# Value products of a cached-attention side stream issued in pairs behind its score products, and empty steps added to an mLSTM side stream

## The chip, the cores and the metric

One core of one Trainium2 chip runs the whole program as one launch. The metric is the device time of that core in microseconds (us).

## The reference, cut to what matters

One decoder layer is applied to 2048 new prompt tokens and to 64 sampled tokens (8 sequences of 8). It projects the tokens once, runs two groups of heads, and then an output projection and an MLP with layer norms. All data are float32.

```python
# sampled tokens, forgetting attention over a paged cache of 8192 past tokens, 8 heads of 64
k_past = cache_k[l][page_table].reshape(DB, past, FOX_HEADS, FOX_HEAD_DIM)
v_past = cache_v[l][page_table].reshape(DB, past, FOX_HEADS, FOX_HEAD_DIM)
s_past = einsum('bqhd,bkhd->bhqk', q, k_past) * scale + Ln[..., :, None] + R[:, :, None, :]
s_new  = einsum('bqhd,bkhd->bhqk', q, k_new) * scale + Ln[..., :, None] - Ln[..., None, :]
p = softmax(concatenate([s_past, where(causal, s_new, -inf)], -1))
o = einsum('bhqk,bkhd->bqhd', p[..., :P], v_past) + einsum('bhqk,bkhd->bqhd', p[..., P:], v_new)
...
# mLSTM, 4 heads of 128, one chunk (the prompt is scanned in chunks, a sample is one chunk)
C_new = g_state * C + einsum('bhs,bshd,bshe->bhde', w_key, k, v)     # state
n_new = g_state * n + einsum('bhs,bshd->bhd', w_key, k)              # normaliser
...
x1 = layer_norm(DN_ALPHA * x + mix @ w_o)
y  = layer_norm(DN_ALPHA * x1 + square(relu(x1 @ w1)) @ w2)
```

## The kernel before

**Main work.** Four stages follow each other: A (input projections of four blocks of 512 prompt tokens; the sampled tokens ride with the first), B (forgetting attention of the prompt), O (output projection) and C (the MLP, again in four blocks). A float32 product of the main work is split into a high and a low part, so that it becomes three matrix products (`mm3`, L157 to L159) of 128 rows by 256 to 512 columns. These are most of TensorE's instructions, and are called big matmuls below.

**Two side streams run beside it.** They are Python generators. The main work calls `tick(us)` after each of its units; `tick` adds `us` to two accounts, and each time an account passes its pace, the generator of that account takes one step (up to its next `yield`).

- The *m stream* (`macc`, pace `PACE_M` = 2.3) holds a list: `gate_stream(bi)` (gate rows of block bi), `m_block(bi)` (the mLSTM chunks of block bi, four chunks of 128 tokens, seven or eight steps each) and, after block 0, `m_sample()` (the mLSTM of the sampled tokens). When block bi+1 reaches its convolutions, it steps the m stream until `m_block(bi)` is done (`while mst.get("open")` in `block_a`), and only then goes on.
- The *attention stream* (`sample_attention`, pace 5.6 in stage A and 5 in stages O and C, nearly none in B) does the sampled tokens' attention over the cache. It has 294 steps; 32 of them belong to one of the 8 samples.

**The attention stream's step n** (`step(n)`) holds, in this order: turning gathered keys on VectorE (`k_turn`, L1674); every fourth step the scores of four gathered key pieces (`qk_step`, L1697: 16 products in 128x32 tiles); once a sample the softmax (`softmax`, L1716 and the exponentials L1734); every second step one value product (`pv_step` of p, L1809: 8 products in 128x32 tiles, p = 0 to 127, 16 to a sample); the end of a sample (`pv_end`, L1824); the new tokens' part (`softmax_new`, L1746) and the sum (`softmax_sum`, L1754); transposes of the weights (`weights(b, u, hg)`, L1766, two calls for each fourth of a sample, copied by ScalarE and VectorE at L1768); and at its end the gathers for later steps (`v_gather`, L1785, and `k_gather`, L1668, indirect DMAs issued by GpSimd).

A value product needs its gathered values in SBUF. There are two places for them: place 0 (two `vt` buffers) always, place 1 only while the main work lends buffers (`vx["more"]`, from stage O on, given back at each block's end). `v_gather` runs when a place is free, on odd steps, or at once when no place is in use. Scores fall on steps n with n % 4 == 2, value products with even p on the same steps behind the scores, and those with odd p on n % 4 == 0.

**The order on each engine** is written when the program is built: the Tile framework takes the instructions with their order of issue as a priority and places each by its own estimate of when its operands are ready. Within an engine that order is fixed at run time. So a step given later in the program moves an instruction only if the framework's estimate did not already put it there.

Of the kernel before, what the change touches and what calls it, by code (L numbers as in the profile page):

```python
# [52 lines left out]
def body(ctx, tc, I, O, stages):  # L53
# [51 lines left out]
    vx = dict(more=None, live=[], next=0, of={})  # L105
# [255 lines left out]
    def gate_stream(bi):  # L361
# [43 lines left out]
        def rowset(cols, base, n_el, np_, sample):  # L405
            R = [pa.tile([8, 1024], F32, name="rows", tag="xn", bufs=2) for _ in range(2)]
            fr = R[1][:, 0:n_el]
            yield 1
            V.tensor_copy(fr, rows([c[0] for c in cols], 8, np_))
            if sample:  # L410
                V.tensor_tensor_scan(fr, rm8, fr, 0.0, op0=OP.mult, op1=OP.subtract)
            else:
                V.tensor_tensor_scan(fr, ones8.to_broadcast([8, 512]), fr, 0.0 if bi == 0 else Lend, op0=OP.mult, op1=OP.subtract)
                V.tensor_copy(Lend, fr[:, 511:512])
            SY.dma_start(dnl[:, base:base + n_el], fr)
            ir = R[0][0:4, 0:n_el]
            yield 1
            V.tensor_copy(ir, rows([c[1] for c in cols], 4, np_))
            lr = R[0][0:4, 512:512 + n_el]
            yield 1  # L420
            V.tensor_copy(lr, rows([c[2] for c in cols], 4, np_))
            mr = R[1][0:4, 0:n_el]
            br = R[1][0:4, 512:512 + n_el]
            if sample:
                V.tensor_tensor_scan(br, rm8[:4], lr, 0.0, op0=OP.mult, op1=OP.add)
                for b in range(8):
                    s = slice(b * 8, b * 8 + 8)
                    V.tensor_tensor_scan(mr[:, s], lr[:, s], ir[:, s], smT[:, b:b + 1], op0=OP.add, op1=OP.max)
                m0 = [smT[:, b:b + 1] for b in range(8)]
                cl = 8  # L430
                mo = O["m_sample"].rearrange("l b h -> h (l b)")
            else:
                for c in range(4):
                    s = slice(c * 128, c * 128 + 128)
                    V.tensor_tensor_scan(br[:, s], ones8[:4].to_broadcast([4, 128]), lr[:, s], 0.0, op0=OP.mult, op1=OP.add)
                V.tensor_tensor_scan(mr, lr, ir, 0.0 if bi == 0 else mend, op0=OP.add, op1=OP.max)
                cl = 128

            V.tensor_tensor(lr, mr, br, op=OP.subtract)
            V.tensor_tensor(ir, ir, br, op=OP.subtract)  # L440
            SY.dma_start(dM[:, base:base + n_el], lr)
            for c in range(n_el // cl):
                s = slice(c * cl, c * cl + cl)
                if sample:
                    m0 = smT[:, c:c + 1]
                elif c == 0:
                    m0 = None if bi == 0 else mend
                else:
                    m0 = mr[:, c * cl - 1:c * cl]
                if m0 is None:  # L450
                    V.tensor_scalar(br[:, s], lr[:, s], -1.0, None, op0=OP.mult)
                else:
                    V.tensor_scalar(br[:, s], lr[:, s], -1.0, m0, op0=OP.mult, op1=OP.add)
            SY.dma_start(dar[:, base:base + n_el], br)
            ge = pa.tile([4, 8], F32, name="ge", bufs=1)[:, :n_el // cl]
            V.tensor_copy(ge, br.rearrange("p (c t) -> p c t", t=cl)[:, :, cl - 1])
            if sample:
                SY.dma_start(dgs_s, ge)
                me = pa.tile([4, 8], F32, name="me", bufs=1)
                V.tensor_copy(me, mr.rearrange("p (c t) -> p c t", t=cl)[:, :, cl - 1])  # L460
                SY.dma_start(mo, me)
            else:
                SY.dma_start(dgs[:, bi * 4:bi * 4 + 4], ge)
                V.tensor_copy(mend, mr[:, 511:512])
                if bi == 3:
                    SY.dma_start(O["m_prompt"].rearrange("l b h -> h (l b)"), mend)
            if bi == 0 and not sample:
                yield 1

            for i, c in enumerate(cols):  # L470
                yield 1
                s = slice(i * np_, (i + 1) * np_)
                pg = ppm.tile([128, 8], F32, name="mg", tag="mm", bufs=2)[:np_]
                T.transpose(pg[:, 0:4], ir[:, s], ident[:4, :4])
                T.transpose(pg[:, 4:8], mr[:, s], ident[:4, :4])
                V.tensor_copy(c[3], pg)
# [3 lines left out]
        if pre:  # L480
            yield from rowset([(gnats[:, 0:8], gats[:, 8:12], gnats[:, 8:12], gms)], S, 64, 64, True)
# [342 lines left out]
    def m_sample():  # L824
# [67 lines left out]
        for h in range(4):  # L892
# [32 lines left out]
            for q in range(2):  # L925
                vx = pm.tile([64, 4, 128], F32, name="vx", tag="va", bufs=2)
                V.tensor_tensor(vx, va[:, h, None, 0:128].to_broadcast([64, 4, 128]),
                                bm[:, q * 4:q * 4 + 4, None].to_broadcast([64, 4, 128]), op=OP.mult)
                yield 1
                pc = ppm.tile([128, 4, 128], F32, name="mm", tag="mm", bufs=2)  # L930
                T.matmul(pc, kw[:, h], vx, start=True, stop=True)
                for b in range(4):
                    bb = q * 4 + b
                    V.scalar_tensor_tensor(C0[:, bb], C0[:, bb], gsb[:, h, bb:bb + 1], pc[:, b], op0=OP.mult, op1=OP.add)
# [3 lines left out]
            T.matmul(pn2, kw[:, h], bm, start=True, stop=True)  # L938
            V.tensor_tensor(n1[:, :, h], n0[:, :, h], gsb[:, h], op=OP.mult)
            V.tensor_tensor(n1[:, :, h], n1[:, :, h], pn2, op=OP.add)  # L940
        yield 1
        pe = ppm.tile([32, 128], F32, name="mm", tag="mm", bufs=2)
        T.transpose(pe, n1.rearrange("p b h -> p (b h)"), ident)
# [587 lines left out]
def sample_attention(tc, I, O, ps_, pps, cst, ident, sqk, dnl, dR, dmix, dqb, vx, kx, pe, ring_a):  # L1531
# [84 lines left out]
    for g in range(2):  # L1616
        p = pps.tile([32, 8, 64], F32, name="sT", tag="sX", bufs=1)
# [174 lines left out]
    def pv_step(b, kt, after):  # L1792


        z = state[b]
        if kt == 0:
            z["po"] = pps.tile([128, 256], F32, name="sO", bufs=1)
        po = z["po"]
        pg = kt % 4
        vts = vx["of"].pop(b * 16 + kt)  # L1800
        vx["live"].pop(0)
        for n, f in enumerate((1, 0)):
            with ExitStack() as es:
                if after is not None:
                    es.enter_context(tc.issue_after(after.ins))
                for g in range(2):
                    for hg in range(2):
                        r = (g * 2 + hg) * 32
                        after_ = T.matmul(po[r:r + 32], z["PT"][:, hg, 2 * f + g, pg].rearrange("p h q -> p (h q)"),  # L1809
                                          vts[f][:, g, hg * 256:(hg + 1) * 256], start=(kt == 0 and n == 0),  # L1810
                                          stop=(g == 1 and kt == 15 and n == 1), skip_group_check=True)
            after = after_
        if kt == 15:
            for hg in range(2):
                T.matmul(po[hg * 32:hg * 32 + 32], z["pn"][:, hg], z["vn"][:, hg * 256:(hg + 1) * 256],
                         start=False, stop=True, skip_group_check=True)
            z["os"] = ps_.tile([128, 256], F32, name="os", bufs=1)
            V.tensor_scalar(z["os"], po, z["rl"], None, op0=OP.mult)

    def pv_end(b):  # L1820
        z = state.pop(b)
# [11 lines left out]
    def at(n, first, of):  # L1833

        i, r = divmod(n - first, of)
        return i if r == 0 and i >= 0 else None
# [4 lines left out]
    def step(n):  # L1841
        after = None
# [11 lines left out]
        if g is not None and g < 64:  # L1854
            after = qk_step(g)
        b = at(n, 35, 32)
        if b is not None and b < 8:
            softmax(b)
        p = at(n, 38, 2)
        if p is not None and p < 128:  # L1860
            pv_step(p // 16, p % 16, after)
        b = at(n, 69, 32)
        if b is not None:
            pv_end(b)
        b = at(n, 37, 32)
        if b is not None and b < 8:
            softmax_new(b)
            v_new(b)
        b = at(n, 40, 32)
        if b is not None and b < 8:  # L1870
            softmax_sum(b)
        for hg in range(2):
            u = at(n, 36 + hg, 8)
            if u is not None and u < 32:
                weights(u // 4, u % 4, hg)
        b = at(n, 30, 32)
        if b is not None and b < 7:
            q_load(b + 1)
        b = at(n, 3, 32)
# [12 lines left out]
        if NA + 6 <= n < 256:  # L1892
            k_gather(n)

    for n in range(294):
        yield 1
        step(n)
        if n == NA + 2:

            yield 3  # L1900
            for i in range(6):
                k_gather(NA + i)
                if i < 5:
                    yield 1
# [23 lines left out]
```

## Time and profile before

| | |
|---|---|
| time, median of 3 runs | 3322.77 us (3321.24 to 3331.57) |
| the profiled execution's own time | 3348.73 us, of which its span is 3347.0 us |
| granted TensorE clock over the span | 0.989 |
| instructions in the span | 57284 |

A page of the profile gives each engine's busy time; a group of instructions (line of the kernel, engine, operation, output<-inputs) gives a count, the busy time, the mean of one, and the idle time of the engine just before the group with what ended it. PE is TensorE's matmul, PEld its weight load, DVE is VectorE, ACT ScalarE, POOL GpSimd. A float32 product in a 128x32 tile leaves two records, so the 8 products of a `pv_step` show as x16 and the 16 of a `qk_step` as x32. In a timeline, a row's first number is its start, and the step from one start to the next is what an instruction costs TensorE, because durations overlap.

### The profile page before, as it was taken

Reading aid. Unit: us, or ns where it says so; the run is one execution under the profiler, and the core shown is the slowest. Engines: PE = TensorE matmul, PEld = TensorE weight load, DVE = VectorE, ACT = ScalarE, POOL = GpSimd, SP = SyncE. Lnnn points to the kernel's source line nnn. Section 1 sums busy time; section 2 is a strip of 40 time slices with the busy share of each in tenths; the row PEclk is TensorE's granted clock in tenths of the full one; section 3 lists DMA queues with packets and bytes.
Section 4 is the critical chain, followed back from the end, with each engine's and each line's share of the span. In section 5 each row is a group of like instructions: output and inputs, shape, how many; then the busy total and the mean of one; then the engine's idle time right before and its main releaser. Section 6 shows DMA issues by size and latency. Waiting matters only on the chain. (4 is left out here: it accounts for less than half of the span.)

```text
span 3347.0 us, 57284 instructions
## 1 busy us (share of the span) xinstructions
PE 3224.8 (96%) x21420; PEld 2634.7 (79%) x21420; DVE 2130.2 (64%) x5161; ACT 1355.5 (40%) x2670; POOL 929.7 (28%) x1060
## 2 busy tenths in 40 slices
PE   9999999999999999999999999999999999999998
PEld 8998897787877777676777777777776777889997
DVE  6857567556478777656666667666676545755555
ACT  4443344334367777312332333232332333433332
POOL 0112122322344444465323324323243210100001
PEclk9999999999999999999999999999999999999999
DMA  5666765867642223787877768767668654542221
GB/s 174 167 190 190 220 205 189 288 215 226 220 122 84 77 82 114 246 274 242 296 241 250 247 232 298 253 224 270 211 238 304 198 172 142 160 138 79 89 85 66
DMA packets 427294, 646.22 MB, mean 193 GB/s; under 512 B 83149, under 2 KB 320017, under 8 KB 426121
## 3 DMA queue, kind: packets, MB, share of 16 engines
q1 hardware_dynamic: 350184, 363.09, 35.9%
q0 software_dynamic: 74304, 270.57, 22.0%
q10 hardware_dynamic: 2528, 8.91, 0.7%
q8 instruction: 169, 2.77, 0.3%
q14 instruction: 109, 0.89, 0.1%
HBM read 589.63 MB, written 52.83 MB: 192 GB/s over the span
## 5 line engine op out<-in xcount | busy, mean ns | idle before, releaser
L1489 DVE TENSOR_TENSOR y<-y,py 128x512 f32<-128x512 f32 x475 | 320.6, 682 | 313.5 <-PE py L159 276.9
L149 ACT ACTIVATE wh<-wr 128x1024 fp32r<-128x1024 f32 x268 | 279.4, 1056 | 523.7 <-PE py L159 207.1
L1668 POOL DMA_INDIRECT kT<-cache_k,idxK x256 | 269.1, 1051 | 725.5 <-PE sQ L1697 657.7
L159 PE MATMUL ph<-x1h,wl 128*128 128x512 f32 (+1 forms) x1280 | 452.6, 355 | 9.5 <-DVE wl L152 8.3
L157 PE MATMUL ph<-x1h,wh 128*128 128x512 f32 (+1 forms) x1280 | 454.7, 355 | 4.0 <-ACT wh L149 2.2
L158 PE MATMUL ph<-x1l,wh 128*128 128x512 f32 (+1 forms) x1280 | 454.5, 355 | 1.6 <-issue 1.6
L1674 DVE STREAM_TRANSPOSE kT<-kT 128x512 f32<-128x512 f32 x512 | 330.3, 685 | 182.2 <-DMA kT<-cache_k,idxK 171.6
L157 PE MATMUL py<-wh,h 128*128 128x512 f32 x1024 | 407.0, 400 | 4.4 <-DVE y L1487 2.3
L159 PE MATMUL py<-wh,h 128*128 128x512 f32 x1024 | 401.6, 393 | 1.0 <-issue 1.0
L158 PE MATMUL py<-wl,h 128*128 128x512 f32 x1024 | 401.5, 393 | 1.1 <-issue 1.0
L152 DVE TENSOR_TENSOR wl<-wr,wh 128x1024 fp32r<-128x1024 f32 x268 | 336.8, 1263 | 89.2 <-PE ph L159 35.2
L157 PE MATMUL pm<-whi,xhT 128*128 128x256 f32 (+2 forms) x1040 | 303.4, 292 | 3.2 <-issue 2.0
L158 PE MATMUL pm<-wlo,xhT 128*128 128x256 f32 (+2 forms) x1040 | 298.1, 287 | 0.0
L159 PE MATMUL pm<-whi,xlT 128*128 128x256 f32 (+2 forms) x1040 | 297.9, 286 | 0.0
L159 PEld LDWEIGHTS ph<-x1h,wl 128*128 128x128 f32 x1280 | 241.7, 189 | 45.6 <-DVE wl L152 10.5
L157 PEld LDWEIGHTS ph<-x1h,wh 128*128 128x128 f32 x1280 | 241.5, 189 | 42.0 <-issue 4.7
L158 PEld LDWEIGHTS ph<-x1l,wh 128*128 128x128 f32 x1280 | 241.8, 189 | 37.8 <-issue 6.4
L157 PEld LDWEIGHTS py<-wh,h 128*128 128x128 f32 x1024 | 192.5, 188 | 59.4 <-issue 11.9
L159 PEld LDWEIGHTS py<-wh,h 128*128 128x128 f32 x1024 | 192.5, 188 | 46.9 <-issue 5.8
L158 PEld LDWEIGHTS py<-wl,h 128*128 128x128 f32 x1024 | 192.7, 188 | 37.4 <-issue 2.3
L1785 POOL DMA_INDIRECT vt<-cache_v,idxV x158 | 161.5, 1022 | 201.0 <-PE sO L1809 140.2
L157 PEld LDWEIGHTS pm<-whi,xhT 128*128 128x128 f32 (+1 forms) x1040 | 199.1, 191 | 11.5 <-issue 8.8
(420 smaller groups left out, 6627.5 us busy)
## 6 DMA issues: line engine op xcount, KB each, us to landing
wr<-w SPq DMA_DIRECT2D x256, 512.0 KB
wra<-w_in SPq DMA_DIRECT2D x112, 512.0 KB
Rb<-dR SPq DMA_DIRECT2D x128, 128.0 KB
wr<-w_o SPq DMA_DIRECT2D x16, 512.0 KB
xr<-dmix SPq DMA_DIRECT2D x16, 512.0 KB
y<-x_prompt SPq DMA_DIRECT2D x16, 512.0 KB
dx<-y SPq DMA_DIRECT2D x16, 512.0 KB
xr<-dx SPq DMA_DIRECT2D x16, 512.0 KB
```

The source lines that it names most:

```text
L149: last["ACT"] = A.activation(dst, src, AF.Copy, scale=scale)
L152: r = (eng or V).tensor_tensor(dst, src, hi.bitcast(F32), op=OP.subtract)
L157: T.matmul(ps, wh, xh, start=first, stop=False)
L158: T.matmul(ps, wh, xl, start=False, stop=False)
L159: last["PE"] = T.matmul(ps, wl, xh, start=False, stop=stop)
L1489: V.tensor_tensor(y, y, ps, op=OP.add)
L1668: G.indirect_dma_start(out=piece(n), out_offset=None, in_=ck, in_offset=IO(ap=idxK[:, b, j // 2, j % 2:j % 2 + 1], axis=0))
L1674: V.transpose(x, x)
L1785: G.indirect_dma_start(out=vt.rearrange("p f c -> p (f c)"), out_offset=None, in_=cv, in_offset=IO(ap=idxV[:, b, (kt % 4) * 4 + kt // 4, f ...
```

## The change

Attention stream: a value product with even p is followed in the same step by the one with odd p, if its gather has been issued; `done` remembers how far the products have come, so that the odd one is not done again. Products whose partner has not been gathered are done alone as before. The new tokens' part moves from step 37 to 39 of a sample, the sum from 40 to 41, and both transposes of a sample's first fourth go to step 37 (they were at 36 and 37).

m stream: one more empty step in `gate_stream` of block 0, ahead of the transposes of its prompt rows; one ahead of each of the eight state products of `m_sample` (four heads, two halves); one ahead of its normaliser's transpose.

```diff
             if bi == 0 and not sample:
+                yield 1
                 yield 1
...
                 V.tensor_tensor(vx, va[:, h, None, 0:128].to_broadcast([64, 4, 128]),
                                 bm[:, q * 4:q * 4 + 4, None].to_broadcast([64, 4, 128]), op=OP.mult)
                 yield 1
+                yield 1
                 pc = ppm.tile([128, 4, 128], F32, name="mm", tag="mm", bufs=2)
                 T.matmul(pc, kw[:, h], vx, start=True, stop=True)
...
+        yield 1
         yield 1
         pe = ppm.tile([32, 128], F32, name="mm", tag="mm", bufs=2)
         T.transpose(pe, n1.rearrange("p b h -> p (b h)"), ident)
...
             V.tensor_scalar(z["os"], po, z["rl"], None, op0=OP.mult)
+        return after
...
         p = at(n, 38, 2)
-        if p is not None and p < 128:
-            pv_step(p // 16, p % 16, after)
+        if p is not None and p < 128 and p >= done[0]:
+            after = pv_step(p // 16, p % 16, after)
+            done[0] = p + 1
+            if p % 2 == 0 and p + 1 in vx["of"]:
+                pv_step(p // 16, p % 16 + 1, after)
+                done[0] = p + 2
...
-        b = at(n, 37, 32)
+        b = at(n, 39, 32)
         if b is not None and b < 8:
             softmax_new(b)
             v_new(b)
-        b = at(n, 40, 32)
+        b = at(n, 41, 32)
         if b is not None and b < 8:
             softmax_sum(b)
         for hg in range(2):
             u = at(n, 36 + hg, 8)
-            if u is not None and u < 32:
+            if u is not None and u < 32 and u % 4:
                 weights(u // 4, u % 4, hg)
+            u = at(n, 37, 32)
+            if u is not None and u < 8:
+                weights(u, 0, hg)
...
+    done = [0]
     for n in range(294):
         yield 1
         step(n)
```

## The prediction

> **What bounds the kernel.** I read the page first, for the engine that is full; then the groups of the lines that the change touches, by whole run and in stage A alone; then the timeline of TensorE around single bursts of the attention stream, since the page's averages can't price a change of order; and last the instruction order of both kernels as built, which tells what moves.
>
> ```profile
> span 3347.0 us, 57284 instructions
> ...
> PE 3224.8 (96%) x21420; PEld 2634.7 (79%) x21420; DVE 2130.2 (64%) x5161; ACT 1355.5 (40%) x2670; POOL 929.7 (28%) x1060
> ```
>
> TensorE is busy for 96% of the span and no other engine comes near. Every instruction keeps its work, so time can only come from two places: the idle 122 us (3347.0 less 3224.8), or the extra steps that TensorE spends where it goes over from one kind of product to another.
>
> The groups, each with its count, busy time, mean, and the idle time just before it with what ended it; the first row is of the stretch from 240 to 915 us alone, the others of the whole run:
>
> ```profile
> L1809 PE MATMUL sO<-vt,PTs 128*32 128x256 f32 x336 | 26.3, 424 | 15.8 <-DMA vt<-cache_v,idxV 15.8
> ...
> L1809 PE MATMUL sO<-xr,PTs 128*32 128x256 f32 x672 | 47.9, 382 | 0.6 <-DMA xr<-cache_v,idxV 0.6
> L1809 PE MATMUL sO<-vx,PTs 128*32 128x256 f32 x112 | 7.3, 380 | 0.0
> L1766 PE MATMUL sT<-ident,S 128*128 128x128 f32 x256 | 40.8, 280 | 7.4 <-ACT S L1734 4.1 <-ACT PTs L1768 2.9 <-DVE mxs L1704 0.3
> L931 PE MATMUL mm<-vx,kws 64*128 64x512 f32 x16 | 9.0, 641 | 2.2 <-DVE vx L927 1.7 <-ACT num L916 0.5
> L943 PE MATMUL mm<-ident,n 128*32 128x128 f32 x1 | 0.3, 284 | 1.8 <-DVE n L940 1.8
> L474 PE MATMUL mg<-ident,rows 4*128 4x4 f32 (+1 forms) x17 | 3.0, 209 | 2.4 <-DVE rows L440 2.4
> L802 PE MATMUL mn<-va,kw 128*128 128x129 f32 x128 | 19.5, 275 | 3.4 <-ACT hh L728 1.8 <-issue 1.6
> ```
>
> Sixteen records make one value product. In stage A 21 products (336 records) run with one place only, and there TensorE waits 15.8 us for their gathers, 0.75 us each. From the lent buffers (xr and vx) come 42 + 7 = 49 products with 0.6 us of waits: where two places exist, the values are there in time. The new order has 50 pairs, all in stages O and C, and leaves the 28 others alone; so the pairing does nothing for the 15.8 us.
>
> **Pairs.** What a product costs alone, between big matmuls:
>
> ```profile
> 2262.41 0.39 PE L159 MATMUL ph<-x1h,wl 128*128 128x512 f32 x1
> 2262.72 1.07 PE L1809 MATMUL sO<-xr,PTs 128*32 128x256 f32 x16
> 2263.72 0.50 PE L157 MATMUL py<-wh,h 128*128 128x512 f32 x1
> 2264.07 0.40 PE L158 MATMUL py<-wl,h 128*128 128x512 f32 x1
> 2264.31 0.40 PE L159 MATMUL py<-wh,h 128*128 128x512 f32 x1
> 2264.54 0.40 PE L157 MATMUL py<-wh,h 128*128 128x512 f32 x1
> 2264.77 0.40 PE L158 MATMUL py<-wl,h 128*128 128x512 f32 x1
> ```
>
> and what it costs as the second of a pair behind scores, which happens by chance already:
>
> ```profile
> 2432.90 1.93 PE L1697 MATMUL sQ<-kT,qb 128*32 128x256 f32 x32
> 2434.65 1.05 PE L1809 MATMUL sO<-vt,PTs 128*32 128x256 f32 x16
> 2435.51 1.05 PE L1809 MATMUL sO<-xr,PTs 128*32 128x256 f32 x16
> 2436.49 0.50 PE L159 MATMUL py<-wh,h 128*128 128x512 f32 x1
> ```
>
> Read the starts. The plain step of a big matmul is 0.23 (2264.54 to 2264.77). Going into the lone product takes 0.31, the product 1.00, the first big matmul behind it 0.35. From 2262.41 to 2264.77 it is 2.36 us; less five plain steps (1.15), 1.21 us. In the pair the product steps from 2434.65 to 2435.51, and the way out is as long as it is behind a lone one: 0.86 us. So a lone product that is moved behind another saves 0.35 us.
>
> How many move: in the old order 67 runs of value products start straight behind a big matmul, in the new one 35. That is 32 x 0.35 = 11.2 us. Against this, weight transposes that used to stand behind the odd product are now entered from a big matmul (20 stood behind a product, now 4):
>
> ```profile
> 2405.93 0.39 PE L158 MATMUL ph<-x1l,wh 128*128 128x512 f32 x1
> 2406.16 0.60 PE L1766 MATMUL sT<-ident,S 128*128 128x128 f32 x4
> 2406.52 0.48 PE L159 MATMUL ph<-x1h,wl 128*128 128x512 f32 x1
> 2406.83 0.40 PE L157 MATMUL py<-wh,h 128*128 128x512 f32 x1
> ...
> 2284.40 0.66 PE L1766 MATMUL sT<-ident,S 128*128 128x128 f32 x4
> 2284.81 0.47 PE L157 MATMUL ph<-x1h,wh 128*128 128x512 f32 x1
> 2285.12 0.39 PE L158 MATMUL ph<-x1l,wh 128*128 128x512 f32 x1
> ```
>
> Alone, the transposes take 0.36 and the big matmul behind them 0.31 instead of 0.23: 0.44. Behind a product they take 0.41, and the big matmul behind them 0.31 where it would be 0.35 behind the product: 0.37. So 16 x 0.07 = 1.1 us come back, and 10.1 remain. A second count gives the lower end: all interruptions of the big matmuls, whoever makes them, go from 544 to 521, and 23 x 0.35 = 8.1. I take 9, with 8.1 and 10.1 as ends.
>
> What else hangs on it: the two gathers that follow are issued together. On GpSimd this is hardly new; the framework had already put four key gathers and both value gathers in one batch of eight, and the new order of GpSimd's queue differs in few places:
>
> ```profile
> 2104.20 0.94 POOL L1668 DMA_INDIRECT kT<-cache_k,idxK  x1 [18.35 <-PE sQ L1697]
> ...
> 2112.91 0.95 POOL L1785 DMA_INDIRECT xr<-cache_v,idxV  x1 [0.30 <-issue]
> ```
>
> So the key gathers and the turns on VectorE behind them keep their times, and the second product of a pair loses only the half period by which it used to come later. I put its new waits at 0; the upper end is the third rival.
>
> **The first weights of a sample.** Their two transposes were in step 36, right behind the softmax of step 35, and waited twice for its exponentials:
>
> ```profile
> 538.43 0.66 PE L1766 MATMUL sT<-ident,S 128*128 128x128 f32 x4 [1.90 <-ACT S L1734]
> ...
> 539.81 0.63 PE L157 MATMUL pm<-xhT,whi 128*128 128x512 f32 x1
> 540.24 0.63 PE L158 MATMUL pm<-xlT,whi 128*128 128x512 f32 x1
> ...
> 1517.36 0.65 PE L1766 MATMUL sT<-ident,S 128*128 128x128 f32 x4 [2.20 <-ACT S L1734]
> ```
>
> In the new order the first stands 7 big matmuls later (7 x 0.23 = 1.6 us) and the second 29 (6.7 us). So 1.6 of the 1.90 and all of the 2.20 can go. There is a second price in these rows: behind the wait a 512-column matmul steps 0.43 (539.81 to 540.24), nearly twice the plain 0.23, for about eight matmuls; with the first wait some 8 x 0.2 = 1.6 us go too. That is 5.4 at most; nothing if the exponentials are late by as much again. I take 4.
>
> The Trainium skill bears on that second price: its page "TensorE: Matmul & The Clock Gate", section "What's actually happening", says that TensorE's clock falls to half after at least one idle window of about 3.4 us. By that page a wait of 1.90 us need not cost any clock, and this term would be 2.4 us instead of 4. The trace shows the slow steps behind 1.90 us, so the rows decide.
>
> **Empty steps.** The three waits at which they aim are in the rows: L474 2.4, L931 2.2, L943 1.8, together 6.4 us. But the order decides whether they move. In the new order all eight state products and the normaliser's transpose stand between the same two big matmuls as before: the framework had put them later than their steps, where it expects their operands, and what an empty step adds is taken up there. So I put this part at 0. For the gate rows, the 64-token transposes at which TensorE waits stand 6 big matmuls later, but the rows that feed them are turned 13 to 14 later, and VectorE's chain between them is as long: 0, between -1 and +1.
>
> What does move is what is queued behind these steps in the m stream: nine steps at pace 2.3 are 20.7 us, and `m_block(1)` starts that much later. Before, its last step was issued just as block 2 came to its convolutions. Now the whole last chunk is forced there at once, eight steps, and its matmuls stand within 50 big matmuls (11 us) instead of 130 shorter ones. Behind it on VectorE and ScalarE are the convolutions of block 2, and TensorE waits for those. The trace has no such forced chunk of this block; the nearest row is L802's, 1.8 us for ScalarE. Ends: 0, and four such waits, 7 us. As `m_block(1)`'s first chunks stand about as close together in the old order with one such wait, I take 2.
>
> **The sum.** -9 for the pairs, -4 for the weights, 0 for the targets of the empty steps, +2 for the late chunk: -11 us. The profiled execution's own time is 3348.73, of which 1.7 lie outside the span; it would become 3337.7. It stands 26 us above the median of the runs shown, and none of my terms depends on what made it slower, so I take the 11 us off the median: 3322.8 - 11 = 3312. The terms' ends give -16.5 (10.1, 5.4 and 1) to 0 (8.1 against 7 and 1).
>
> **Rivals.**
>
> The first: *the gain is real and is taken up elsewhere.* Where so many instructions of TensorE change places, ScalarE's and VectorE's queues change too, and a wait of 2 us with its slow clock costs some 3.6. For it: the idle 122 us are many single waits. Against: stage B and everything up to 70 us and from 2820 us on keep their order. Two new waits of this size and the late chunk at its upper end: -13 + 7.2 + 7 = +1, say 3322.
>
> The second: *the empty steps do remove their waits.* 6.4 us and two spells of slow clock (3.2) more, 9.6: 3302. For it: the row of L931 shows VectorE as late, and a change of its order could free it. Against: the same neighbours in the order.
>
> The third ends slower: *the second product of each pair waits for its gather.* The place is TensorE at the second half of each of the 50 pairs; big matmuls queue behind it. For it: the eight gathers of the batch take GpSimd 9.7 us to issue (2104.20 to 2113.86), and the values still have to land when the next scores come. Against: 0.6 us in 42 products today. If each of the 50 pairs waited as a product of stage A does, 0.75 us, that would be 37.5 us, and 3349. It decides from 0.22 us for each pair (11 / 50); half of stage A's wait gives 18.8 - 11 = +8, and at 0.5 each +14, which I take for this case: 3337. The Trainium skill gives its cause: "DMA: Bandwidth & Descriptors", section "Issuing engines are not separate DMA queues", says that DMAs of all issuing engines share the same 16 DMA engines and interleave; by that rule the weight loads would stretch a batch of value gathers. No row of before shows a pair's wait.
>
> **Chances.** 0.3% of the median, 10 us, is about what a measurement of this kernel can tell from no change. My forecast gets 0.50; it straddles that bound, and I count 0.30 of it as faster and 0.20 as same. The first rival gets 0.22, the second 0.15, the third 0.13 (0.11 of it slower, the rest same). Faster 0.45, same 0.44, slower 0.11. The range: below, it reaches past the second rival's 3302 to 3299; above, over the first rival to 3331, short of the third, with some 0.2 outside on both sides together. The likeliest case alone gives 3306 to 3322.
>
> **What would show it.** Right: L1809's runs behind scores show x32 in one row and lone ones almost only in stage A; L1809's waits stay near 17 us, all of them on vt and in stage A; L1766's 4.1 us for ScalarE's exponentials shrink to below 1; L931 and L943 still wait about 2 us each; between 480 and 530 us TensorE has at most one or two new waits at L711, L794 or L802. Wrong: waits of L1809 for xr or vx of more than 5 us in total; new waits of big matmuls for VectorE behind late key turns (L1674); a time above 3323, or one below 3303, which would need waits to go that I left standing.

## The result, and the profile after

The changed kernel takes 3346.36 us (median of 15 runs, 3328.48 to 3351.65) against 3330.46 us for the kernel before (15 runs, 3321.24 to 3341.13): a ratio of 1.0047, interval 1.0036 to 1.0058, some 16 us slower. Measured again later it was 1.0054 (1.0037 to 1.0071) and 1.0043 (1.0028 to 1.0057). The forecast was 11 us faster, with a range that ended at 3331; it stood on the median of three runs of the kernel before, 3322.8, which lies 8 us below the median of all 15, so it is the loss of 16 us that has to be explained. Runs that share their runs of the kernel before are called a sitting below; there were six, and since before itself stood at 3329 to 3330 us in four of them and at 3342 and 3350 us in two, every time is compared inside its own sitting.

The page after, its engine totals:

```profile
span 3348.9 us, 57288 instructions
...
PE 3220.5 (96%) x21420; PEld 2648.0 (79%) x21420; DVE 2122.6 (63%) x5161; ACT 1359.7 (41%) x2670; POOL 930.8 (28%) x1060
```

TensorE is busy 4.3 us less than in the first profile (3224.8) and idle 128.4 us instead of 122.2. The groups that answer to those of before (whole run; lines are some three higher now):

```profile
L1812 PE MATMUL sO<-vt,PTs 128*32 128x256 f32 x1248 | 88.0, 391 | 22.9 <-DMA vt<-cache_v,idxV 22.9
L1812 PE MATMUL sO<-xr,PTs 128*32 128x256 f32 x688 | 47.3, 381 | 1.1 <-DMA xr<-cache_v,idxV 1.0
L1769 PE MATMUL sT<-ident,S 128*128 128x128 f32 x256 | 40.5, 281 | 16.0 <-ACT PTs L1771 12.8 <-ACT y L175 3.2
...
L933 PE MATMUL mm<-vx,kws 64*128 64x512 f32 x16 | 9.6, 684 | 3.5 <-DVE vx L928 3.5
...
L475 PE MATMUL mg<-ident,rows 4*128 4x4 f32 (+1 forms) x17 | 3.1, 210 | 2.4 <-DVE rows L440 2.4
L946 PE MATMUL mm<-ident,n 128*32 128x128 f32 x1 | 0.3, 272 | 0.0
```

The weight transposes (L1766 before, 7.4 us of idle time) now wait 16.0 us. The 4.1 us that they waited for ScalarE's exponentials are gone, as forecast; in their place stand 12.8 us for ScalarE's copies of weights. A new wait of one down-projection matmul is as long as any of them. TensorE's rows in the timeline, and then ScalarE's ahead of them:

```profile
2462.06 0.80 PE L157 MATMUL py<-wh,h 128*128 128x512 f32 x1 [6.88 <-ACT h L149]
2462.66 0.63 PE L158 MATMUL py<-wl,h 128*128 128x512 f32 x1
2463.08 0.63 PE L157 MATMUL py<-wh,h 128*128 128x512 f32 x1
```

```profile
2432.72 0.25 ACT L1751 COPY PTn<-sT 8x32 f32<-8x32 f32 x2 [10.71 <-PE sT L1749]
2435.52 0.60 ACT L1454 ACTIVATE hq<-ph 128x512 f32<-128x512 f32 x1 [2.54 <-PE ph L159]
2436.15 0.63 ACT L1455 ACTIVATE hq<-hq 128x512 f32<-128x512 f32 x1
2439.42 0.63 ACT L149 ACTIVATE h<-hq 128x512 fp32r<-128x512 f32 x1 [2.64 <-PE py L159]
2439.96 2.96 ACT L149 ACTIVATE wh<-wr 128x1024 fp32r<-128x1024 f32 x3
2459.15 1.06 ACT L149 ACTIVATE wh<-wr 128x1024 fp32r<-128x1024 f32 x1 [16.23 <-DMA wr<-w]
2460.11 0.58 ACT L1454 ACTIVATE hq<-ph 128x512 f32<-128x512 f32 x1
2460.72 0.63 ACT L1455 ACTIVATE hq<-hq 128x512 f32<-128x512 f32 x1
2461.38 0.63 ACT L149 ACTIVATE h<-hq 128x512 fp32r<-128x512 f32 x1
```

Read ScalarE's rows as a queue. Four weight splits (`wh<-wr`) stand in a row, and the fourth waits 16.23 us for its load. Behind it stand `hq`, `hq` and `h`, whose input from TensorE was there long before; TensorE needs that `h`. The queue begins with the two small copies of the new tokens' weights (`PTn`), ahead of which ScalarE stood idle for 10.71 us. They were over 2.5 us before the first `hq` could start, and that `hq` waited for TensorE. So the copies hold up nothing in these rows; what counts is the order that the build wrote behind them, three splits and the late one ahead of the next `hq`, `hq` and `h`.

The first profile of before was of a run 26 us above its median, so a profile of before taken in the same sitting as a third one of the change is the better pair. The engine totals of the two, before and then after (first lines of their pages):

```profile
span 3332.7 us, 57284 instructions
...
PE 3221.7 (97%) x21420; PEld 2637.8 (79%) x21420; DVE 2130.8 (64%) x5161; ACT 1357.0 (41%) x2670; POOL 932.6 (28%) x1060
```

```profile
span 3337.7 us, 57288 instructions
...
PE 3215.0 (96%) x21420; PEld 2647.3 (79%) x21420; DVE 2121.2 (64%) x5161; ACT 1358.5 (41%) x2670; POOL 927.1 (28%) x1060
```

Here the change saves 6.7 us of busy TensorE time and adds 11.7 us of idle time (111.0 to 122.7). The profiled runs differ by 5.5 us, the medians of their sitting by 13.3; the profiled run of before lies 2.8 us above the median of its kernel and that of the change 2.7 below, so the traces show less than the medians. The group of the weight transposes in the same two profiles:

```profile
L1766 PE MATMUL sT<-ident,S 128*128 128x128 f32 x256 | 40.3, 277 | 3.9 <-ACT PTs L1768 1.9 <-ACT S L1734 1.8 <-PE sO L1809 0.2
```

```profile
L1769 PE MATMUL sT<-ident,S 128*128 128x128 f32 x256 | 41.0, 284 | 19.2 <-ACT PTs L1771 13.8 <-DVE mixs L1833 5.5
```

That is 15.3 us more in this one group, and the down-projection's wait is 7.4 us in this profile. All three profiles of the change have the waits near 2462 (6.9, 6.4, 7.4 us), 2536 (3.3, 5.3, 4.7), 558 (7.4, 7.0, 6.8) and 1526 (3.2, 5.9, 5.5; again at transposes of weights, behind `y` or `mixs`). The two profiles of the old order in sittings with before near 3330 (the second with four extra transposes at its start, below) have no wait of more than 2.8 us at any of these places.

### The profile page after: what moved, and what is told of

Same layout as the page of the kernel before. It is cut to its first block, busy times and chain, and to the rows that moved or that the text cites. A ratio compares the mean times of both kernels' runs of the same rounds, so it can differ in the third digit from the quotient of the medians.

```text
span 3348.9 us, 57288 instructions
## 1 busy us (share of the span) xinstructions
PE 3220.5 (96%) x21420; PEld 2648.0 (79%) x21420; DVE 2122.6 (63%) x5161; ACT 1359.7 (41%) x2670; POOL 930.8 (28%) x1060
```

## Experiments

**The two halves.** The attention stream's edits alone, and the three kinds of empty steps alone. The instruction orders show that the one half leaves the m stream in place and the other leaves the attention stream in place, all but the first weights of one sample.

> The attention stream's part of the change alone: pairs of value products, the new values, sums and first weights later; no empty steps. The side stream keeps its order. By the prediction's terms: -9 for the pairs and -4 for the first weights, -13 us (0.4% faster). Theory 1 (the empty steps make the change slower, by delaying gate_stream(2) and the last chunk of m_block(1) against a block 2 that does not move): this kernel keeps the gain or some of it, between -13 and 0 us. Theory 2 (the attention part makes it slower, by weight loads and gathers that meet at the ends of the MLP blocks, as in the 7.0 us wait of the down-projection at 2462): +10 to +20 us, as the whole change.

> The three kinds of empty steps alone, the attention stream as before. Theory 1: +10 to +25 us (the whole change's +16 and, if the attention part gains, its 9 to 13 on top), and ScalarE waits several us for the loads of block 2's gate rows near 550 us, as in the whole change. Theory 2: within 4 us of before.

Measured: attention part 3396.72 against 3341.78 us, 1.0166 (1.015 to 1.0182), +55 us; empty steps 3334.39, 0.9979 (0.9968 to 0.9989), -7 us. Theory 1 falls. But the whole change is +16, so the parts do not add up.

**The attention part split in two.** Pairs alone:

```diff
-        if p is not None and p < 128:
-            pv_step(p // 16, p % 16, after)
+        if p is not None and p < 128 and p >= done[0]:
+            after = pv_step(p // 16, p % 16, after)
+            ...
```

> The pairs alone: the second value product of a pair behind the first, nothing else moved. By the prediction's term -9 us (-8.1 to -10.1), with runs of value products that start behind a big matmul down from 67 to 38. Theory 1: -9 to 0 us. Theory 2: if the pairs carry the loss (each waits for its gather, 50 pairs at 0.5), +14 us and new waits of the value products on the lent buffers; if the moved weights and sums carry it, this kernel shows -9 and the one with the moves alone the loss.

The other moves alone (new tokens' part 37 to 39, sum 40 to 41, first weights both at 37):

> The moves alone: new values and their softmax two steps later, the sums one step later, both first weights of a sample in one step; products one by one as before. By the prediction's term -4 us (0 to -5.4), the weight transposes' waits for ScalarE's exponentials down from 4.1 us to below 1. Theory 1: -5 to +2 us. Theory 2: up to +16 us if the later sums and weights hold up what comes behind them.

Measured: pairs 1.0081 (1.0061 to 1.0101), +25 us; moves 1.0064 (1.0047 to 1.0081), +26 us by the medians and +21 by the ratio. Neither gain showed. The profiles of this sitting have something that the one of the change has hardly any of: TensorE idle for nothing that the profile shows. The scores of the new keys in the attention part alone (timeline; 32 records of small matmuls that are one burst of 0.44 us elsewhere):

```profile
2420.57 0.36 PE L1716 MATMUL sQ<-qt,qb 128*32 128x8 f32 x18
2421.56 0.28 PE L1716 MATMUL sQ<-qt,qb 128*32 128x8 f32 x4 [0.63 <-issue]
2422.28 0.17 PE L1716 MATMUL sQ<-qt,qb 128*32 128x8 f32 x1 [0.45 <-issue]
2423.02 0.23 PE L1716 MATMUL sQ<-qt,qb 128*32 128x8 f32 x2 [0.57 <-issue]
2423.74 0.17 PE L1716 MATMUL sQ<-qt,qb 128*32 128x8 f32 x1 [0.49 <-issue]
2425.14 0.23 PE L1716 MATMUL sQ<-qt,qb 128*32 128x8 f32 x2 [1.23 <-issue]
```

**Does that time belong to the program?** The whole change again; then the kernel before and the attention part, each with four transposes more at the very start. These change the place of every later instruction in TensorE's stream and, in the built order, no other instruction of any engine.

```diff
+            for j in range(lead):          # 4 on the first call, then 0
+                T.transpose(px[:, j % 4], ident, ident)
             for k in range(4):
                 T.transpose(px[:, k, :n], ...)
```

> The whole change once more, beside the kernel before and the attention part on the same chip. The parts measured +55 us (attention part alone) and -7 us (empty steps alone), yet the whole change +16. If parts add up, this run is near +48 us. If the whole change really keeps 30 us that the attention part alone loses, it is again near +16 (+10 to +20), and its profile again shows hardly any idle time of TensorE that ends for nothing the profile shows (2 us, against 26 us in the attention part alone and 13 us in the profile of before).

> The kernel before with four extra transposes of the identity at the very start, where TensorE waits 4.7 us for the first rows anyway. Every other instruction of every engine keeps its place in its engine's order. Theory 3 (where TensorE's instructions lie, or how they are fetched, sets how often it waits for nothing that the profile shows): the time moves by 5 to 30 us in either direction, and the waits that end with issue change place or sum. Theory 4 (the order of the instructions alone sets the time): within 4 us of before, the same waits at the same places.

> The attention part alone, with the same four extra transposes at the start; no other instruction moves. Theory 3: the time moves away from that of the attention part alone (+55 us) by 10 to 40 us, most likely down, because its 26 us of waits that end with issue go or shrink. Theory 4: again +55 us within 6 us, with about 26 us of such waits, 13 us of them at the scores of the new keys.

Measured, with before at 3329.52: the change 1.0054 (+21 us), the shifted kernel before 1.0008 (0.9994 to 1.0021), the shifted attention part 1.0061 (1.0042 to 1.0081, +21 us). Either the four transposes had taken 30 us away from the attention part, or the sitting had. In the same sitting:

> Only the softmax over new keys two steps later and its sums one step later; first weights, products and side stream as before. The moves together cost +26 us. If they cost by their place in the order (theory 4), this half carries +26 or the first weights do, and the waits of TensorE name it (the transposes of the new weights, their sums). If by theory 3, this kernel lies anywhere between -10 and +30 us, with the difference in waits that end with issue and in the slow steps behind them.

Measured: 3344.07, 1.0047 (1.003 to 1.0065), +15 us for two small moves of the new tokens' part. This is the size of the whole loss.

**Repeats and the first weights alone.**

> The attention part alone, unchanged, a second time. It measured +55 us on a chip where the kernel before also stood 12 us higher than on the next one; with four extra transposes at the start it measured +21 us on that next chip. Theory 5 (the idle time of TensorE that ends for nothing the profile shows belongs to the chip that a run falls on, not to the place of the instructions): on a chip where before is near 3330, this kernel is near +20 us with under 8 us of such waits; on one where before is near 3342, near +55 with some 25. Theory 3 (the place of the instructions): near +55 on any chip.

> The pairs alone, a second time, for another chip (+25 us on the first). Theory 5: lower, +8 to +15 us on a chip with before near 3330: 34 batches of eight gathers in place of 22 hold up weight loads at the ends of MLP blocks, with ScalarE late at the weights' transposes near 2536 (6.8 us there in the first run). By the prediction's term: -9 us.

> The moves alone, a second time (+26 us on the first chip). The later softmax and sums alone measured +15 us on a chip with before near 3330. Theory 5: +12 to +20 us here on such a chip, with TensorE's waits of some 3 us each for key turns and values near 582 and 617, which the kernel before does not have. By the prediction's term: -4 us.

> The first weights of a sample alone in their later step; new values, sums, products and side stream as before. By the prediction -4 us (0 to -5.4). If the loss of the moves is in the later softmax and sums alone, this kernel lies at -5 to +2 us; if the weights carry part of it, at +5 to +15 us, with new waits of TensorE for ScalarE's copies of the weights.

Measured, with before at 3349.53: attention part 1.0172 (+58 us), pairs 1.01 (+32), moves 1.0085 (+26), first weights 1.0003 (0.9992 to 1.0015). The first weights cost nothing and bring nothing. The other three were again in a sitting with such idle time; TensorE's waits in the attention part:

```profile
PE sO L1809 <- DMA vt<-cache_v,idxV: 19.2, 7, 4.3
PE sQ L1716 <- issue: 16.0, 23, 1.9
```

**The place of the instructions, or the sitting?** Side by side at last:

> The kernel before itself, for a profile in the same sitting as the next three; its time is that of before (ratio 1, within 0.2%). In the sittings where before took 3330 us (two of them) the profiles held 0 to 9 us of TensorE's idle time that ends for nothing the profile shows, in those where it took 3342 and 3350 us 11 to 42 us. If that is a state of the sitting (theory 5), this profile has 10 us or more of it when before is over 3340, and under 5 when it is near 3330.

> The attention part alone, a third time. Theory 3 (where the instructions lie): +55 us in this sitting too, whatever before takes, while the same kernel with four transposes more at the start is at +21. Theory 5 (the sitting): the same as that one within 6 us: both near +21 if before is near 3330, both near +55 if it is above 3340.

> The attention part alone with four transposes of the identity more at the start, a second time, now beside the one without them. Theory 3: +21 us, with under 8 us of idle time that ends for nothing the profile shows. Theory 5: as its neighbour without the four, within 6 us.

> The whole change, a third time, beside the attention part alone in the same sitting. From 1612 us on both have every instruction of every engine in the same order. Theory 3: +16 to +20 us as before, 35 us below the attention part alone. Theory 5: within 8 us of the attention part alone (the empty steps gave -7): near +15 in a sitting with before near 3330, near +45 in one above 3340.

Measured, with before at 3329.25: before itself 1.0002 (0.9989 to 1.0014); attention part 3349.37, 1.0057 (1.0038 to 1.0076), +20 us; with four transposes more 3355.33, 1.0081 (+26); whole change 3342.56, 1.0043 (+13). So the same attention part takes +20 in one sitting and +55 and +58 in others: theory 3 falls, and theory 5 holds as a statement on the sitting. Its first form, by the chip, had fallen already: before took 3330 us in one sitting and 3350 in the next on the same chip. The idle time that ends with "issue" sums to between 0 and 9.3 us in the profiles of the four quieter sittings, and to between 7.9 and 33.1 in those of the other two (12.6 in the first profile of before, whose run was 26 us above its median). The same burst of small matmuls in the attention part's profile of this sitting:

```profile
2378.53 0.44 PE L1716 MATMUL sQ<-qt,qb 128*32 128x8 f32 x32
```

**Which edit carries the 13 to 20 us.** The whole change less the later softmax:

```diff
-        b = at(n, 39, 32)      # softmax_new, v_new
+        b = at(n, 37, 32)
...
-        b = at(n, 41, 32)      # softmax_sum
+        b = at(n, 40, 32)
```

> The whole change less one edit: the softmax over new keys and its sums at their old steps (37 and 40); pairs, first weights and empty steps as in the change. Theory 6 (the later softmax of the new keys carries the loss: ScalarE's two small copies of it stand ahead of weight splits, VectorE's low halves come late behind them, SyncE waits for those at the layer norm's loads, and the next weight loads go out behind sixteen gathers): the 6.4 to 7.4 us wait of the down-projection near 2462 is gone, and the time lies at 0 to +5 us against before, with the pairs' -7 us of steps kept. Theory 7 (the pairs' batches of eight gathers carry it): +10 to +16 us as the whole change, with the waits near 2462 and near 2536 still there.

Measured: 3332.58 against 3330.21, ratio 0.9998 (0.9983 to 1.0013). The loss is gone with this edit, and it appears (+15) with this edit alone. Theory 7 falls: from stage O on, with a pause of 1.5 us as the end of a batch, this kernel's trace has 36 batches of eight gathers, the change 34, the kernel before 17 and 22 in its two profiles, and it is not slower. ScalarE's rows for the stretch in question, in this kernel:

```profile
2422.41 2.20 ACT L149 ACTIVATE wh<-wr 128x1024 fp32r<-128x1024 f32 x2 [10.59 <-PE py L159]
2425.45 0.60 ACT L1454 ACTIVATE hq<-ph 128x512 f32<-128x512 f32 x1 [0.84 <-PE ph L159]
2426.09 0.63 ACT L1455 ACTIVATE hq<-hq 128x512 f32<-128x512 f32 x1
2426.75 0.64 ACT L149 ACTIVATE h<-hq 128x512 fp32r<-128x512 f32 x1
2427.89 1.07 ACT L149 ACTIVATE wh<-wr 128x1024 fp32r<-128x1024 f32 x1 [0.50 <-PE ph L158]
2436.00 0.60 ACT L1454 ACTIVATE hq<-ph 128x512 f32<-128x512 f32 x1 [7.04 <-DVE h L152]
2436.63 0.63 ACT L1455 ACTIVATE hq<-hq 128x512 f32<-128x512 f32 x1
2437.30 0.64 ACT L149 ACTIVATE h<-hq 128x512 fp32r<-128x512 f32 x1
2446.90 1.06 ACT L149 ACTIVATE wh<-wr 128x1024 fp32r<-128x1024 f32 x1 [8.97 <-DMA wr<-w]
```

The late weight split is still there and still waits for its load, at the same moment (2446.90; in the change's profile of the sitting before 2446.99). But `hq`, `hq` and `h` stand ahead of it, and TensorE does not wait. The two SyncE loads went out no earlier (2437.11 and 2439.17, against 2436.13 and 2439.57 in the change). So theory 6 was right about the edit and wrong in its last links: not a later load, but the order of ScalarE's queue, in which weight splits stand ahead of `h`. The other three waits of the change are gone as well: near 550 it is 2.7 us, near 1520 and 2525 nothing over 2.1. TensorE's idle time is 114.2 us here, against 122.7 in the third profile of the change and 111.0 in that of before.

The edit alone (+15) shows no wait near 2462. It has 3.4 us at key turns near 582, and 5.4 us for a load of `xr` near 2455; the latter also stands in the first weights alone (6.5 us), which are no slower than before, so it is not what costs. Its longest wait is 7.46 us at scores, which the profile puts down to nothing. ScalarE's rows ahead of it, and TensorE's:

```profile
2494.30 0.60 ACT L1451 ACTIVATE hq<-ph 128x512 f32<-128x512 f32 x1 [0.94 <-PE ph L159]
2501.63 1.06 ACT L149 ACTIVATE wh<-wr 128x1024 fp32r<-128x1024 f32 x1 [6.73 <-DMA wr<-w]
2502.59 0.61 ACT L1452 ACTIVATE hq<-hq 128x512 f32<-128x512 f32 x1
2503.23 0.63 ACT L149 ACTIVATE h<-hq 128x512 fp32r<-128x512 f32 x1
```

```profile
2505.90 3.64 PE L1697 MATMUL sQ<-kT,qb 128*32 128x256 f32 x32 [7.46 <-issue]
```

It is the same picture: a weight split that waits for its load stands between the first `hq` and the `hq` and `h` behind it. VectorE's low half of that `h` starts at 2503.89 after 7.04 us of waiting, and the key turns that the scores read stand behind it (2504.50). In the later profile of before `hq`, `hq` and `h` follow each other there, and TensorE's wait at this place, for the low half of a weight, is 3.8 us. So the edit is shown, by its removal and alone, and in both (the change, and this edit alone) a long wait goes back to a late weight split ahead of `h`. At which places this happens depends on what else is moved, and why the build writes this order for a softmax two steps later is not shown.

**A version without pairs and without the later softmax.**

> Only the first weights' later step and the empty steps: the two parts that did not measure slower alone (+1 and -7 us). If they add up, -6 us (-10 to -2), below both kernels, with the batches of gathers (22 to 24 of eight) and the value products' 67 runs behind big matmuls as before. If the empty steps' -7 us belong to the sitting in which they were measured, 0.

Measured: 3338.87, 1.0025 (1.0014 to 1.0036), +8 us. A miss: empty steps and first weights did not add up to -6. Its profiled run was the fastest of its twelve and does not show the loss. So whether the empty steps gain (-7 alone, in a sitting with much idle time of the unexplained kind) or lose stays open, and no version was faster than before in more than one sitting.

## Why the prediction was wrong, point by point

**The step that failed is a missing term.** The front matter says that the new tokens' part moves from step 37 to 39 and the sum from 40 to 41; the sum of the prediction has no line for it. It is worth about +15 us: 1.0047 alone, and 0.9998 for the change without it. Its instructions are small (two copies of 8x32, 0.25 us for both), and what was asked of each edit was what it costs and what waits for it on TensorE. What it does, in the stretches shown, is change the order of ScalarE's queue.

**The gains failed too.** The other terms together were -11 us, and the change without the later softmax, which has all of them, measured 0 (-6 to +4). So about 15 of the 27 us between forecast and result are the missing term, and the rest is gain that did not become time.

**Pairs, -9 (8.1 to 10.1).** The count was right: runs of value products behind a big matmul went from 67 to 35 in the records. Of the 16 weight transposes that no longer stand behind a product, though, only ten more are entered from a big matmul (45 before, 55 after). The busy time of TensorE fell by 6.7 us in the pair of profiles of one sitting and by 3.9 in the change without the later softmax (3221.7 to 3217.8, across two sittings; 41 runs there), so a saving shows in the busy time and is somewhat smaller. That it stays as time was not shown: the second kernel's idle time rose by 3.2 us (111.0 to 114.2), it measures equal to before, and the pairs alone were measured only in the two sittings with idle time that nothing explains (+25 and +32), so what they cost or bring alone in the others is open.

**First weights, -4.** The waits for exponentials went from 4.1 us to nothing, as said. The time did not: +1 us alone, between -3 and +5. What was late next was not asked.

**Empty steps, 0 for their targets.** L474 (2.4 to 2.4) and L931 (2.2 to 3.5) waited on as forecast; L943's 1.8 us went, against the forecast: it is 0 in all six profiles with the empty steps, and between 0 and 1.9 us in those without.

**Late chunk, +2 (0 to 7).** The shift of the m stream costs at another place than the one priced. The forced chunk's matmuls were looked at; the rows that `gate_stream(2)` sends to memory, which stands behind that chunk and which block 2 reads back at an unmoved step, were not. ScalarE and TensorE in the third profile of the change:

```profile
538.87 1.28 ACT L762 ACTIVATE Wm<-Wm,gm 128x128 f32<-128x128 f32 x4 [0.60 <-DMA Wm<-dM]
...
544.21 0.63 ACT L767 ACTIVATE qa<-qa 128x512 f32<-128x512 f32 x1 [3.96 <-DMA qa<-dar]
550.09 0.21 ACT L755 ACTIVATE gsb<-gsb 128x16 f32<-128x16 f32 x1 [5.24 <-DMA gsb<-dgs]
...
551.76 1.11 PE L1769 MATMUL sT<-ident,S 128*128 128x128 f32 x4 [6.84 <-ACT PTs L1771]
```

ScalarE stands 9 us for two loads, a copy of weights stands behind them, and TensorE waits 6.8 us. Without the empty steps (attention part alone, same sitting) the wait at these transposes is 2.9 us, in before 2.7 at the neighbouring transposes of new keys; the empty steps alone, in another sitting, have 6.75. So against these the empty steps add about 4 us, inside the 0 to 7 that was given, for another reason. They do not always: in the change without the later softmax ScalarE stands for the same two loads (4.16 and 5.04 us), but only one of the two is ahead of the copy that TensorE needs, and TensorE waits 2.7 us. Between 480 and 530 us, where the forecast placed the late chunk, no wait is left at all.

**Rivals.** The first (the gain is taken up by new waits) named the right mechanism, with two new waits of 2 us; there were four of 3 to 7. (Its sum, -13 + 7.2 + 7 on 3322.8, gives 3324, not 3322.) The third (each pair waits for its gather) named the nearest time, 3337, and the wrong place: products from lent buffers waited 1.2 to 2.0 us in all. The Trainium skill's rule behind it ("DMA: Bandwidth & Descriptors", section "Issuing engines are not separate DMA queues": all issuers' transfers share the same engines) is neither shown nor refuted by these runs. More batches of eight gathers did not slow the kernel without the later softmax (36 batches, 0.9998). The second did not happen.

**What was to show it.** Lone value products almost only in stage A, exponentials below 1 us: right. Value products' waits on `vt` near 17 us: 17.6 to 24.3, of which 3 to 8 outside stage A; the two profiles of before have 17.3 and 21.0, with 1.5 and 3.8 outside. New waits of big matmuls for late key turns were named as the sign of an error; the sign came from ScalarE, which the list did not watch.

**A sentence that a count refutes.** One batch of eight gathers was quoted for "hardly new". From stage O on before has 17 and 22 such batches in its two profiles, the change 34. It turned out harmless, but one row had stood for all.

## What to carry to other kernels

Give every moved line a term, the smallest too: an engine takes its instructions in the order that the build wrote, and moving a small one can change that order around it. Here two steps' delay for two copies, 0.25 us for both, cost more than 32 saved changes of tile shape brought in. For a reordering look at the order of each engine that feeds the full one, around each weight load, and ask whether an instruction that waits for a load now stands ahead of one that the full engine needs. When parts of a change don't add up, measure a part twice in different sittings beside the kernel before, ahead of any story.

## What the runs showed of the hardware that was not expected

TensorE can stand idle for nothing that the profile shows, and how much of this there is depends on the sitting. The same attention part, with TensorE's records in the same order, had 16.0 us of such waits at the scores of the new keys alone in one sitting (its second) and none there in another (its third); its cost against before was 58 us there and 20 us here. In the rows of the first such sitting these scores go on in steps of about 0.7 us, with one to four records each. Before itself stood 12 to 20 us higher in those sittings. The chip does not decide it: one sitting of each kind fell on the same chip. What holds up TensorE was not found; four instructions more at its start changed nothing that can be told from the noise (1.0008). The label alone does not prove this kind of wait: the 7.46 us of the later softmax alone carry it too, and go back to ScalarE's queue.

Slow steps follow such waits as they follow any other. Behind the burst shown above the big matmuls step 0.43 us (2428.04 to 2428.47), with a granted clock of 0.50 between 2426 and 2432 us; behind the 6.88 us wait of the change they step 0.43 us as well (2462.66 to 2463.08), against the plain 0.23. So the waits cost twice: between the attention part's second and third profile TensorE's idle time differs by 27.5 us (160.7 and 133.2) and its busy time by 34.5 (3248.2 and 3213.7).
